# Output weights of group A split early and kept in DRAM, their bounds loaded elsewhere, y stored a unit later, the bias mask laid out on the host

## The chip, the cores and the metric

One core of a Trainium2 chip runs the whole program. Its engines work side by side: TensorE (PE) for matrix products, VectorE (DVE), ScalarE (ACT) and GpSimd (POOL) for elementwise work, and SyncE (SP), whose queue issues nearly all transfers of this kernel, in order. The metric is the device time of one execution, in microseconds (us); lower is better.

## The reference

A hybrid attention block with an MLP, for one sequence of 1024 tokens of width 1024, in float32:

```python
n = rms_norm(x, norm1_g)
qa, ka, va, qb, kb, vb = split(n @ w_in)      # widths 512, 128, 128, 512, 512, 512
ya = mixer_a(...)   # 8 heads of 64 on 2 kv heads, window of 3 chunks of 64, ALiBi, learned sinks
yb = mixer_b(...)   # 8 heads of 64, own chunk and the 8 before it,
                    # plus a learned bias by clipped relative position; else NEG_INF
y = concatenate([rms_norm(ya, out_norm_a_g), rms_norm(yb, out_norm_b_g)])
h = x + y @ w_out
u = square(relu(rms_norm(h, norm2_g) @ w_ff1))
return rms_norm(h + u @ w_ff2, final_norm_g)
```

## The kernel before, in words

**Products.** Data are float32. For a product each operand is split into a high and a low piece of a narrower type, and `mm3` makes the product from three matmuls (high with high, high with low, low with high). Splitting a tile is one ACT row for the high piece (a copy to the narrow type) and one DVE or POOL row for the low one (source minus high). Where the narrow type is f16, the operand is first scaled by a power of two, worked out from a bound on its largest element.

**Attention units.** The first 390 us are input projections, attention and the output projection of group A. Attention runs as 32 units in a fixed order, numbered n: A0_0, A0_2, ... A3_6 (n = 0 to 15; four head pairs, each with four units of two token blocks), then B0_0, B1_0, B0_1, B1_1 (n = 16 to 19), B2_0 (n = 20) and so on to B7_0, B6_1, B7_1 (n = 29, 30, 31; head and half of the tokens). Each unit makes scores (`S_B`; in group A `S_A`), takes exponentials (`P_A`, `P_B`, with `nm_` the negated row maxima from DVE and `sm_` the sums), turns them around (in A by PE transposes `pt_A`, copied by ACT and DVE into `T_A`; in B by a transposing DMA from `H_B`, the pieces of P, into `G_B`) and multiplies by V (`av_A`, `av_B`; the sums go to `Y`). Between the units' matmuls a filler puts the matmuls of the input projections of later heads (`ip_kB`, `ip_qB`, `ip_vB`), and during the last B units those of the output projection of group A (`op_A`). Heads of group B come in pairs: kB1, qB1, vB1 are the projections of pair 1 (heads 2 and 3), KkB, QqB and VvB their keys, queries and values with both pieces.

**Buffers and order.** Weights land in a ring of three load buffers (`stage`, tag "ws"): names `st_qB1`, `bo0` and so on are such buffers. Split pieces (`w0_` high, `w1_` low) and other large tiles live in a ring of 33 pages (`page`). PE's order is written out by the program (`pe` chains every matmul to the one before). The order on the other engines, and on SP, is chosen by the scheduler of the tile framework, which simulates the program; it may move a row ahead of or behind where the program states it. Transfers wait on SP for their buffer and their source, and what stands behind a waiting transfer on SP waits too.

**Output weights.** `w_out` has eight blocks of 128 rows, m = 0 to 3 for group A and 4 to 7 for group B. For the scale of its f16 pieces the kernel needs each row's sum of squares: `bound_weights(m)` loads block m into `bo{m}`, at the start of unit n = m + 2 (`BOUND_AT`), and at the start of the unit after it ACT squares and sums it (L970). `scale_of_weights(0)` turns the sums of group A into a scale at unit B2_0 (DVE rows, and one PE transpose `all_o0` through a PSUM buffer), `scale_of_weights(1)` those of group B at B7_0. `out_weight(m)` loads the block again (`st_o{m}`) and splits it into `w_o{m}` by two ACT rows (L1004) and two DVE rows (L1005); blocks 0 to 3 at the start of the output projection of group A, 4 to 7 in the last unit.

**y.** A finished half of a pair's Y is scaled into f16 pieces (ACT and POOL) and, for pairs 0 to 5, stored to DRAM at once (`yd`). `load_y(m)` brings both token halves back in one transfer of 512 KB ahead of the output projection.

**Bias of group B.** `bias_b[s]` (names `b_B0`, `b_B1`) holds a head's band of biases, 128 x 640. It is loaded (`load_bias`) and then two 64 x 64 corners are set to NEG by POOL (`mask_bias`, L707 and L708), eight times each. DVE adds it to the scores (L660, L662).

## Time and profile before

| | |
|---|---|
| median of 3 runs | 1057.29 us (1055.38 to 1059.46) |
| the profiled execution | 1060.3 us |
| its span | 1058.5 us |
| PE busy | 1004.1 us, 95% of the span |
| DVE, ACT, POOL busy | 72%, 67%, 41% |
| granted TensorE clock, mean | 0.98 |

In the rows of the timeline a line reads: start, duration, engine, line of the kernel, operation, output <- inputs with sizes, count, and in brackets how long the engine stood idle before it and what it waited for. Buffer numbers are left out there: `w_qB` is any of w0_qB0 to w1_qB3. PEld is the weight load of TensorE, which runs beside its matmuls. DMA issues stand under SPq with the time their issue took; from there to landing it takes some microseconds more.

### The profile page before, as it was taken

Reading aid. Unit: us, or ns where it says so; the run is one execution under the profiler, and the core shown is the slowest. Engines: PE = TensorE matmul, PEld = TensorE weight load, DVE = VectorE, ACT = ScalarE, POOL = GpSimd, SP = SyncE. Lnnn points to the kernel's source line nnn. Section 1 sums busy time; section 2 is a strip of 40 time slices with the busy share of each in tenths; the row PEclk is TensorE's granted clock in tenths of the full one; section 3 lists DMA queues with packets and bytes.
Section 4 is the critical chain, followed back from the end, with each engine's and each line's share of the span. In section 5 each row is a group of like instructions: output and inputs, shape, how many; then the busy total and the mean of one; then the engine's idle time right before and its main releaser. Section 6 shows DMA issues by size and latency. Waiting matters only on the chain.

```text
span 1058.5 us, 14063 instructions
## 1 busy us (share of the span) xinstructions
PE 1004.1 (95%) x4821; PEld 566.8 (54%) x4821; DVE 758.4 (72%) x1296; ACT 704.4 (67%) x1118; POOL 432.2 (41%) x324
## 2 busy tenths in 40 slices
...
GB/s 353 259 201 152 130 96 123 198 206 186 203 247 237 164 268 120 120 21 139 200 290 257 183 244 248 186 203 272 242 334 384 219 159 140 178 139 120 1 1 159
DMA packets 150279, 200.63 MB, mean 190 GB/s; under 512 B 78656, under 2 KB 96192, under 8 KB 150208
## 3 DMA queue, kind: packets, MB, share of 16 engines
...
q8 instruction: 38, 0.62, 0.2%
q14 instruction: 33, 0.27, 0.1%
...
## 4 chain that ended last, share of the span: by engine, by line
PE 35%; ACT 9%; DVE 9%; issue 5%; DMA 4%; POOL 2%; SPq 0%; DVEq 0%; ACTq 0%; POOLq 0%
PE f_a L174 13%; PE f L174 8%; PE f_c L174 7%; PE f_b L174 4%; PE op_B L174 2%; POOL W L1428 2%; DMA u<-ud 2%; ACT w L1393 1%; DVE T L1400 1%; DMA m<-in_w_ff_dram 1%; ACT W L1426 1%; DVE X L1316 1%; ACT k L1490 1%; DVE tops_w L1208 1%; ACT k L1489 1%
## 5 line engine op out<-in xcount | busy, mean ns | idle before, releaser
L174 PE MATMUL f<-X,W 128*128 128x512 f16 x1344 | 297.2, 383 | 7.0 <-POOL W L1428 4.8
L174 PEld LDWEIGHTS <-U 128*128 128x128 f16 x1356 | 133.1, 98 | 166.3 <-issue 9.0
L174 PEld LDWEIGHTS <-W 128*128 128x128 f16 x1344 | 132.1, 99 | 168.0 <-POOL W L1428 7.9
L1428 POOL TENSOR_TENSOR U<-u,U 128x1024 f16<-128x1024 f32 x48 | 116.5, 2437 | 173.8 <-ACT U L1426 159.8
L174 PE MATMUL f_a<-V,U 128*128 128x512 f16 x756 | 165.3, 379 | 1.0 <-DVE C L1743 1.0
L1428 POOL TENSOR_TENSOR W<-T,W 128x1024 f16<-128x1024 f32 x29 | 67.9, 2344 | 88.3 <-ACT W L1426 88.3
L1428 POOL TENSOR_TENSOR W<-w,W 128x1024 f16<-128x1024 f32 x21 | 51.6, 2456 | 98.6 <-ACT W L1426 98.6
L174 PE MATMUL f_c<-V,U 128*128 128x512 f16 x384 | 86.5, 386 | 5.5 <-DVE V L1430 3.4
L1424 ACT ACTIVATE u<-u,uup 128x1024 f32<-128x1024 f32 x48 | 53.9, 1141 | 56.1 <-DMA u<-ud 55.9
L1430 DVE SCALAR_TENSOR_TENSOR V<-Z,up,V 128x1024 f16<-128x1024 f32 x32 | 51.4, 1610 | 28.7 <-ACT V L1426 18.5
L663 ACT ACTIVATE P_B<-P_B,nm_B 128x640 f32<-128x640 f32 (+2 forms) x64 | 44.3, 692 | 40.2 <-DVE nm_B L660 23.5
L1426 ACT ACTIVATE U<-u 128x1024 f16<-128x1024 f32 x48 | 50.2, 1046 | 28.1 <-DVE Z L1400 10.8
L901 DVE SCALAR_TENSOR_TENSOR H_B<-P_B,rc_B,H_B 128x640 f16<-128x640 f32 (+2 forms) x64 | 51.3, 823 | 14.3 <-ACT H_B L896 13.9
L174 PEld LDWEIGHTS <-y 128*128 128x128 f16 x384 | 36.6, 100 | 41.8 <-DVE ts_vB L477 3.6
L174 PE MATMUL ip_kB<-nT,w_kB 128*128 128x512 f32 x192 | 54.9, 412 | 2.0 <-POOL w_kB L180 1.3
L1430 DVE SCALAR_TENSOR_TENSOR V<-w,up,V 128x1024 f16<-128x1024 f32 x24 | 42.5, 1771 | 19.7 <-ACT V L1426 15.6
L174 PE MATMUL ip_qB<-nT,w_qB 128*128 128x512 f32 x192 | 55.3, 415 | 1.2 <-ACT P_B L663 1.2
L174 PE MATMUL op_A<-w_o,y 128*128 128x512 f16 x192 | 51.5, 395 | 3.4 <-DVE ts_vB L477 3.4
L174 PE MATMUL S_B<-KkB,QqB 128*128 128x320 f32 (+2 forms) x192 | 44.1, 339 | 10.4 <-DVE nm_B L662 6.8
L174 PE MATMUL ip_qA<-nT,w_qA 128*128 128x512 f32 x192 | 52.8, 411 | 0.3 <-DVE VA L180 0.3
L174 PE MATMUL ip_vB<-nT,w_vB 128*128 128x512 f32 x192 | 51.2, 400 | 0.0
L1426 ACT ACTIVATE V<-Z,up 128x1024 f16<-128x1024 f32 x32 | 36.5, 1139 | 21.6 <-DVE Z L1400 19.4
...
## 6 DMA issues: line engine op xcount, KB each, us to landing
w<-in_w_ff_dram SPq DMA_DIRECT2D x64, 512.0 KB, 7.0
u<-ud SPq DMA_DIRECT2D x56, 512.0 KB, 5.4
ud<-k SPq DMA_DIRECT2D x48, 512.0 KB, 3.1
m<-in_w_ff_dram SPq DMA_DIRECT2D x32, 512.0 KB, 6.0
...
xr<-in_x_dram SPq DMA_DIRECT2D x8, 512.0 KB, 8.7
bo<-in_w_out_dram SPq DMA_DIRECT2D x8, 512.0 KB, 3.5
st_o<-in_w_out_dram SPq DMA_DIRECT2D x8, 512.0 KB, 4.8
```

The lines of the kernel that those rows point to most:

```text
L174: pe(nc.tensor.matmul(*args, **kw))
L663: nc.scalar.activation(pr, pr, AF.Exp, bias=nm, scale=-1.0, accum_out=sm)
L901: nc.vector.scalar_tensor_tensor(lo, q, rc, hi, ALU.mult, ALU.subtract)
L1208: nc.vector.tensor_reduce(self.column(), flat(src), mybir.AxisListType.X, ALU.max, apply_absolute_value=True)
L1316: engine.tensor_tensor(lo, src, hi, ALU.subtract)
L1393: nc.scalar.activation(w, w, AF.Copy, scale=up1)
L1400: engine.tensor_tensor(t, a, b, op)
L1424: nc.scalar.activation(full, full, AF.Copy, scale=up)
L1426: nc.scalar.activation(w[0], full, AF.Copy, scale=1.0 if up is None else up)
L1428: engine.tensor_tensor(w[1], full, w[0], ALU.subtract)
L1430: engine.scalar_tensor_tensor(w[1], full, up, w[0], ALU.mult, ALU.subtract)
L1489: nc.scalar.activation(v, v, AF.Relu, scale=down1[n])
```

## The change

- **Bounds.** Blocks 0 to 3 are loaded at n = 3 to 6 (`BOUND_A`), 4 to 7 at n = 13 to 16 (`BOUND_B`), and squared at the start of the unit two later.
- **Pieces of group A.** Their largest bound is found at n = 9 and the scale at n = 10 (`SPREAD_A`). Blocks 0 to 3 are loaded again at n = 9 to 12 (`PIECES_A`, buffers `so{m}`), split two units later, and the pieces stored to DRAM (`wod`, 512 KB a block) one unit after that. The output projection loads them (`w_r{m}`) instead of loading and splitting `st_o0` to `st_o3`. Blocks 4 to 7 are split as before.
- **Scale of group B.** The bound at B7_0, the scale at B6_1, one unit later.
- **y.** Its store is issued a unit later; the second half of the tokens is loaded at the second token block of the output projection instead of with the first.
- **Mask.** The corners are NEG in the band that the host lays out; the 16 rows on POOL go.

```diff
@@ -50,8 +50,8 @@
 Y_UP, Y_DOWN, O_UP = 13, 14, 12
-BOUND_AT = 2
-SPREAD_B = "B7_0"
+BOUND_A, PIECES_A, BOUND_B = 3, 9, 13
+SPREAD_A, SPREAD_B = (9, 10), ("B7_0", "B6_1")
 PAD = 40
@@ -246,6 +246,7 @@
     yd = dram([6, P, 2, 2, HALF], "yd", F16)
+    wod = dram([4, P, 2, D], "wod", F16)
     hB = [dram([P, 2, D], f"hB{n}") for n in range(TB // 2)]
@@ -273,10 +274,14 @@
-    def bits_over(cols, name, psum, tag, bufs, least):
+    def top_over(cols, name):
...
         nc.vector.tensor_reduce(top, cols, mybir.AxisListType.X, ALU.max)
+        return top
+    def bits_over(top, name, psum, tag, bufs, least):
         spread = psum.tile([P, P], F32, tag=tag, bufs=bufs, name=f"all_{name}")
@@ -672,7 +677,14 @@
-    sq = {}
+    sq, late = {}, []
+    def issue_late(units):
+        while late and late[0][0] >= units:
+            late.pop(0)[1]()
+        for work in late:
+            work[0] += 1
@@ -690,7 +702,6 @@
                     self.load_bias(s)
-                    self.mask_bias(s)
                     continue
@@ -702,10 +713,6 @@
             self.bias.append(bias_b[s])
-        def mask_bias(self, s):
-            nc.gpsimd.memset(bias_b[s][:HD, 5 * P - HD :], NEG)
-            nc.gpsimd.memset(bias_b[s][HD:, :HD], NEG)
@@ -728,7 +735,7 @@
             if self.y is None:
-                nc.sync.dma_start(yd[self.m, :, t], y)
+                late.append([0, lambda: nc.sync.dma_start(yd[self.m, :, t], y)])
             if by_act:
@@ -864,21 +871,18 @@
                 defer.pop(0)[1]()
-            if b % 2:
-                self.next_bias(b == 1)
+            if b == 1:
+                self.next_bias()
             if b % 2:
...
-        def next_bias(self, load):
+        def next_bias(self):
             s, j = 1 - self.s, self.pair.j + self.s
...
                 return
-            if load:
-                pairs_b[j].load_bias(s)
-            else:
-                pairs_b[j].mask_bias(s)
+            pairs_b[j].load_bias(s)
@@ -904,6 +908,8 @@
         def step(self, n):
+            if n == 2:
+                issue_late(0)
             self.apply(self.kbs[n])
@@ -942,32 +948,82 @@
-        e = bits_over(topA, "yA", aps, "w", 2, -50)
+        e = bits_over(top_over(topA, "yA"), "yA", aps, "w", 2, -50)
         power(upA, e, -1.0, 254 + Y_UP)
...
-    def scale_of_weights(group):
+    def factors(group):
         c = slice(4 * group, 4 * group + 4)
+        return c, (gains if group else ogc)[:, c]
+    def top_of_weights(group):
+        c, g = factors(group)
         t = small.tile([P, 4], F32, tag="wbound", bufs=2, name=f"wbound{group}")
-        g = ogc[:, c]
         if group:
-            g = gains[:, c]
             nc.vector.tensor_tensor(og2[:, c], g, g, ALU.mult)
         nc.vector.tensor_tensor(t, wsq[:, c], og2[:, c], ALU.mult)
-        e = root_of_bits(bits_over(t, f"o{group}", aps, "w", 2, -80))
+        return top_over(t, f"o{group}")
+    def scale_of_weights(group, top):
+        c, g = factors(group)
+        e = root_of_bits(bits_over(top, f"o{group}", aps, "w", 2, -80))
         up = scale_tile("oup", str(group), 2)
...
+    def load_wout(m, name):
+        st = stage([P, D], f"{name}{m}")
+        load(st, w_out[m * P : (m + 1) * P, :])
+        return st
     def bound_weights(m):
-        st = stage([P, D], f"bo{m}")
-        load(st, w_out[m * P : (m + 1) * P, :])
+        st = load_wout(m, "bo")
         return lambda: nc.scalar.activation(st, st, AF.Square, accum_out=wsq[:, m : m + 1])
+    def split_weights(m, st):
+        w = page([P, 2, D], f"w_o{m}", F16)
+        g = gains[:, m : m + 1]
+        for j in range(2):
+            c = slice(j * HALF, (j + 1) * HALF)
+            in_turn("o", nc.scalar.activation(w[:, 0, c], st[:, c], AF.Copy, scale=g))
+            nc.vector.scalar_tensor_tensor(w[:, 1, c], st[:, c], g, w[:, 0, c], ALU.mult, ALU.subtract)
+        return w
+    def pieces_of_weights(m):
+        st = load_wout(m, "so")
+        def split():
+            w = split_weights(m, st)
+            later.append(lambda: nc.sync.dma_start(wod[m], w))
+        return split
+    later, ahead2 = [], []
+    def weights_chores(n):
+        if later:
+            later.pop(0)()
+        if ahead2 and ahead2[0][0] <= n:
+            ahead2.pop(0)[1]()
+        for at, m0, work in ((BOUND_A, 0, bound_weights), (PIECES_A, 0, pieces_of_weights), (BOUND_B, 4, bound_weights)):
+            if 0 <= n - at < 4:
+                ahead2.append((n + 2, work(m0 + n - at)))
+        if n == SPREAD_A[0]:
+            tops_o[0] = top_of_weights(0)
+        if n == SPREAD_A[1]:
+            scale_of_weights(0, tops_o[0])
+    tops_o = {}
@@ -990,19 +1046,19 @@
         y = page([P, 2, 2, HALF], f"y_{m}", F16)
-        nc.sync.dma_start(y, yd[m])
+        nc.sync.dma_start(y[:, 0], yd[m, :, 0])
         return y
+    def load_rest(m, y):
+        nc.sync.dma_start(y[:, 1], yd[m, :, 1])
     def out_weight(m):
-        st = stage([P, D], f"st_o{m}")
-        w = page([P, 2, D], f"w_o{m}", F16)
-        load(st, w_out[m * P : (m + 1) * P, :])
-        g = gains[:, m : m + 1]
-        for j in range(2):
-            c = slice(j * HALF, (j + 1) * HALF)
-            in_turn("o", nc.scalar.activation(w[:, 0, c], st[:, c], AF.Copy, scale=g))
-            nc.vector.scalar_tensor_tensor(w[:, 1, c], st[:, c], g, w[:, 0, c], ALU.mult, ALU.subtract)
+        if m < 4:
+            w = page([P, 2, D], f"w_r{m}", F16)
+            nc.sync.dma_start(w, wod[m])
+        else:
+            w = split_weights(m, load_wout(m, "st_o"))
         return w[:, 0], w[:, 1]
@@ -1091,6 +1147,9 @@
         for tb in range(TB):
+            if tb == 1:
+                for m in range(4):
+                    load_rest(m, ys[m])
             h = hres[tb] = page([P, D], f"h{tb}", F32)
@@ -1150,20 +1209,22 @@
             scale_of_y()
-    bound = None
     for n, (unit, name, n_fill) in enumerate(units):
-        if bound is not None:
-            bound()
-        bound = bound_weights(n - BOUND_AT) if 0 <= n - BOUND_AT < 8 else None
+        if unit.name[0] == "A" or n == 16:
+            issue_late(1)
+        weights_chores(n)
         if unit.name == "B2_0":
-            scale_of_weights(0)
             rA = group_rstd("A", aps, "w", 2, None)
-        if unit.name == SPREAD_B:
-            scale_of_weights(1)
+        if unit.name == SPREAD_B[0]:
+            tops_o[1] = top_of_weights(1)
+        if unit.name == SPREAD_B[1]:
+            scale_of_weights(1, tops_o[1])
         ahead.remove(unit)
...
                 ys.append(load_y(m) if m < 6 else y67[m - 6])
+                if m < 6:
+                    load_rest(m, ys[-1])
                 ws.append(out_weight(m))
@@ -1904,6 +1965,8 @@
     band = np.stack([ext[:, 127 - p : 127 - p + 640] for p in range(128)], axis=1)
+    band[:, :64, 576:] = NEG
+    band[:, 64:, :64] = NEG
     d = -np.abs(128 + np.arange(128)[:, None] - np.arange(256)[None, :]).astype(np.float32)
```

What the scheduler makes of it at three places. First ACT, around the square of bo0 (`T_A0_0_0` is the first copy of turned probabilities; before, then now):

```order
L413 ACTIVATE ts_qA1_0_688<-ts_qA1_0_688 128x512
L970 ACTIVATE bo0_933,wsq_184<-bo0_933 128x1024
L231 ACTIVATE w0_qA3_811<-st_qA3_810 128x1024
L663 ACTIVATE P_A0_2_1_714,sm_A0_2_668<-P_A0_2_1_714,nm_A0_2_667 128x256 x2
L789 ACTIVATE es_A0_2_723<-nm_A0_2_667,psink_83 128x2
L670 ACTIVATE T_A0_0_0_742<-pt_A0_0_0_741 128x256
L670 ACTIVATE T_A0_0_1_751<-pt_A0_0_1_750 128x512
```

```order
L418 ACTIVATE ts_qA1_0_689<-ts_qA1_0_689 128x512
L231 ACTIVATE w0_qA3_812<-st_qA3_811 128x1024
L668 ACTIVATE P_A0_2_1_715,sm_A0_2_669<-P_A0_2_1_715,nm_A0_2_668 128x256 x2
L796 ACTIVATE es_A0_2_724<-nm_A0_2_668,psink_83 128x2
L988 ACTIVATE bo0_1039,wsq_185<-bo0_1039 128x1024
L675 ACTIVATE T_A0_0_0_743<-pt_A0_0_0_742 128x256
L675 ACTIVATE T_A0_0_1_752<-pt_A0_0_1_751 128x512
```

The square stands three rows further back, still right ahead of T_A. On SP the load of st_kB0 (wk of pair 0) now stands ahead of bo0's, where it stood behind it; each of bo1 to bo3 is loaded into a buffer that the bo before it held.

Second SP where the A units end (VvB0 are the values of pair 0, KkB1x the keys of pair 1, G_B0_0 the turned pieces of unit B0_0). Before; st_qB1 and st_vB1 stand 17 and 7 rows ahead of the first row shown:

```order
L130 DMA st_kB2_2394<-in_w_in_dram 128x1024
L731 DMA yd_88<-y1_2_1901 128x1024
L499 DMA_TRANSPOSE VvB0_1925<-hvB0_1922 128x8x64 x4
L130 DMA st_qB2_2558<-in_w_in_dram 128x1024
L731 DMA yd_88<-y0_3_2100 128x1024
L467 DMA KkB12_2157<-t1_kB1_2028 64x1024 x2
L467 DMA KkB13_2158<-t1_kB1_2028 64x1024 x2
L467 DMA KkB10_2155<-t0_kB1_2029 64x1024 x2
L467 DMA KkB11_2156<-t0_kB1_2029 64x1024 x2
L904 DMA_TRANSPOSE G_B0_0_2128<-H_B0_0_1_2186 128x6x128
L904 DMA_TRANSPOSE G_B0_0_2128<-H_B0_0_3_2230 128x14x128
L904 DMA_TRANSPOSE G_B1_0_2245<-H_B1_0_1_2284 128x6x128
```

Now, in two pieces that follow one another but for row wod of block 3:

```order
L738 DMA yd_88<-y1_2_1919 128x1024
L504 DMA_TRANSPOSE VvB0_1942<-hvB0_1939 128x8x64 x4
L130 DMA st_qB1_1961<-in_w_in_dram 128x1024
L1006 DMA wod_89<-w_o1_1948 128x2048
L130 DMA bo4_2049<-in_w_out_dram 128x1024
L1006 DMA wod_89<-w_o2_2044 128x2048
L130 DMA bo5_2149<-in_w_out_dram 128x1024
L130 DMA st_vB1_2204<-in_w_in_dram 128x1024
```

```order
L472 DMA KkB12_2194<-t1_kB1_2062 64x1024 x2
L908 DMA_TRANSPOSE G_B0_0_2169<-H_B0_0_1_2223 128x6x128
L472 DMA KkB13_2195<-t1_kB1_2062 64x1024 x2
L472 DMA KkB10_2192<-t0_kB1_2063 64x1024 x2
L738 DMA yd_88<-y0_3_2134 128x1024
L130 DMA bo6_2271<-in_w_out_dram 128x1024
L472 DMA KkB11_2193<-t0_kB1_2063 64x1024 x2
L130 DMA bo7_2378<-in_w_out_dram 128x1024
L908 DMA_TRANSPOSE G_B0_0_2169<-H_B0_0_3_2267 128x14x128
L908 DMA_TRANSPOSE G_B1_0_2287<-H_B1_0_1_2326 128x6x128
L908 DMA_TRANSPOSE G_B1_0_2287<-H_B1_0_3_2376 128x14x128
```

The load of st_qB1 has come behind VvB0; in its ring it follows so1 (split into w_o1), and bo4 follows it. Both transfers of G_B0_0 had the keys alone ahead of them; the second now has bo6 and bo7 too. On ACT the square of bo4 now stands directly ahead of T_A3_6_0, and those of bo5, bo6 behind it follow one by one among the rows of B0_0 to B0_1.

Third SP at the start of the output projection of group A, before and now:

```order
L904 DMA_TRANSPOSE G_B4_1_3373<-H_B4_1_1_3426 128x20x128
L993 DMA y_0_3496<-yd_88 128x2048
L993 DMA y_1_3505<-yd_88 128x2048
L993 DMA y_2_3514<-yd_88 128x2048
L703 DMA b_B0_597<-in_relb_dram 128x640
L130 DMA st_o3_3516<-in_w_out_dram 128x1024
L904 DMA_TRANSPOSE G_B4_1_3373<-H_B4_1_3_3475 128x20x128
L993 DMA y_3_3523<-yd_88 128x2048
L130 DMA st_o4_4239<-in_w_out_dram 128x1024
L130 DMA st_o5_4248<-in_w_out_dram 128x1024
L464 DMA QqB30_3412<-t0_qB3_3408 64x512
L464 DMA QqB31_3413<-t0_qB3_3408 64x512
```

```order
L908 DMA_TRANSPOSE G_B4_1_3394<-H_B4_1_1_3446 128x20x128
L1059 DMA w_r0_3510<-wod_89 128x2048
L1049 DMA y_0_3512<-yd_88 128x1024
L1059 DMA w_r1_3514<-wod_89 128x2048
L1049 DMA y_1_3516<-yd_88 128x1024
L1059 DMA w_r2_3518<-wod_89 128x2048
L1049 DMA y_2_3520<-yd_88 128x1024
L1059 DMA w_r3_3522<-wod_89 128x2048
L1049 DMA y_3_3524<-yd_88 128x1024
L908 DMA_TRANSPOSE G_B4_1_3394<-H_B4_1_3_3496 128x20x128
L714 DMA b_B0_598<-in_relb_dram 128x640
L908 DMA_TRANSPOSE G_B5_1_3533<-H_B5_1_1_3567 128x20x128
```

G_B4_1's second transpose and b_B0 have come behind all eight loads, where three loads stood ahead of b_B0. The loads st_o4 to st_o6 stand far ahead now, where st_o0 to st_o2 stood. Of y, `128x2048` has become `128x1024`; the other halves follow some ten rows below, between b_B1 and h1 (rows of x for the residual).

## The prediction

> **What bounds the kernel now.** I read the page's first part, then the list of all waits of PE, then windows by stage, then the timeline of each engine around the waits found.
>
> The page, busy time and share of the span:
>
> ```profile
> PE 1004.1 (95%) x4821; PEld 566.8 (54%) x4821; DVE 758.4 (72%) x1296; ACT 704.4 (67%) x1118; POOL 432.2 (41%) x324
> ```
>
> PE is the bound: 1004.1 of a span of 1058.5, so about 54 us is all that any change of waits can bring, and the change leaves PE's matmuls as they are (their order too, but for one small transpose). The question is which of PE's waits go and which new ones come. PE's waits between 40 and 400 us (total, times, longest):
>
> ```profile
> PE S_B L174 <- DVE nm_B L662: 6.8, 2, 5.4
> PE av_A L174 <- ACT T_A L670: 5.2, 2, 3.5
> PE S_B L174 <- DVE nm_B L660: 3.6, 3, 1.5
> PE op_A L174 <- DVE ts_vB L477: 3.4, 1, 3.4
> PE av_A L174 <- DVE T_A L180: 2.0, 3, 0.9
> PE ss_A L174 <- DVE t_qB L449: 1.3, 1, 1.3
> PE ip_qB L174 <- ACT P_B L663: 1.2, 1, 1.2
> ```
>
> Four of these rows (5.2, 3.6, 3.4 and the 5.4 in 6.8) lie at places that the change touches. The stages, as busy time of each engine in a window (PE, PEld, DVE, ACT, POOL, granted clock, DMA share, GB/s):
>
> ```profile
> 140.00:160.00 20.00, 17.96 (x93) 14.93 (x91) 13.82 (x43) 12.21 (x36) 14.92 (x16) 0.91 0.32 92
> 160.00:180.00 20.00, 17.93 (x97) 14.83 (x96) 14.23 (x38) 13.83 (x36) 13.74 (x14) 1.00 0.33 82
> 180.00:200.00 20.00, 19.12 (x101) 15.53 (x100) 16.30 (x42) 15.17 (x35) 9.28 (x9) 1.00 0.91 193
> 300.00:320.00 20.00, 15.55 (x76) 11.26 (x74) 15.52 (x28) 13.35 (x25) 1.50 (x4) 1.00 1.09 253
> ```
>
> Work is added to the first three, where PE has little slack and ACT is 41.2 of 60 us busy; it is taken from the last, where PE idles 4.5 of 20 us and DMA is full.
>
> **The bounds of the output weights (squares of bo).** Where they stand, on SP, ACT and PE (start, duration, in brackets the idle time before):
>
> ```profile
> 50.28 0.52 SPq L130 DMA_DIRECT2D bo<-in_w_out_dram  x1
> 50.91 0.38 SPq L130 DMA_DIRECT2D st_kB<-in_w_in_dram  x1
> 55.07 1.06 ACT L970 ACTIVATE bo<-bo 128x1024 f32<-128x1024 f32 x1 [5.59 <-DMA bo<-in_w_out_dram]
> 58.66 0.38 PE L174 MATMUL av_A<-T_A,VA 128*128 128x256 f32 x1 [3.48 <-ACT T_A L670]
> 59.79 0.39 PE L174 MATMUL av_A<-T_A,VA 128*128 128x256 f32 x1 [0.75 <-DVE T_A L180]
> 81.14 1.06 ACT L970 ACTIVATE bo<-bo 128x1024 f32<-128x1024 f32 x1 [2.69 <-DMA bo<-in_w_out_dram]
> 85.74 0.38 PE L174 MATMUL av_A<-T_A,VA 128*128 128x256 f32 x1 [1.69 <-ACT T_A L670]
> 86.46 0.62 PE L174 MATMUL av_A<-T_A,VA 128*128 128x256 f32 x3 [0.34 <-DVE T_A L180]
> ```
>
> bo4 to bo7 leave this part of the program altogether. ACT's wait of 2.69 for bo4 goes, and with it the 1.69 + 0.34 = 2.0 us that PE waits four microseconds later: **−2.0** (nothing if another row holds T_A there; I see none). For bo0 the change does less than its words: the scheduler still sets bo0's square right ahead of the T_A copy, only three ACT rows further on, and SP now loads st_kB0 ahead of bo0, so that bo0 lands after 57 instead of 55. Square and T_A then end about where they did: **0**. All of 3.48 + 0.75 = 4.2 could go if bo0 landed as before; the loss if bo1 to bo3, each now loaded only after the square before it, hold ACT in turn is about 1.5 (a late landing of some 2 us, less the rows that run meanwhile).
>
> **The boundary between A and B (150 to 200 us).** What the added pieces cost (count, busy, mean ns):
>
> ```profile
> L1005 DVE SCALAR_TENSOR_TENSOR w_o<-st_o,gains_o,w_o 128x512 f16<-128x512 f32 x16 | 14.8, 966 | 5.6 <-ACT w_o L1004 5.6
> L1004 ACT ACTIVATE w_o<-st_o,gains_o 128x512 f16<-128x512 f32 x16 | 10.3, 713 | 4.0 <-DMA st_o<-in_w_out_dram 4.0
> L970 ACT ACTIVATE bo<-bo 128x1024 f32<-128x1024 f32 x8 | 8.4, 1056 | 8.8 <-DMA bo<-in_w_out_dram 8.7
> L970 ACT ACTIVATION_READ_ACCUMULATOR bo<-bo 128x1 f32 x8 | 1.5, 186 | 0.0
> ```
>
> Eight halves at 0.71 and four squares at 1.06 + 0.19 put 5.7 + 5.0 = 10.7 us on ACT, and eight at 0.97 put 7.7 us on DVE: ACT goes from 41.2 to about 52 of 60, DVE from 44.4 to 52. That fits only if nothing waits, and SP gets twelve transfers of 512 KB (so, wod, bo) in a ring of three load buffers. The rows there now:
>
> ```profile
> 165.47 5.26 SPq L499 DMA_TRANSPOSE VvB<-hvB  x4
> 169.37 1.05 ACT L231 ACTIVATE w_qB<-st_qB 128x1024 fp32r<-128x1024 f32 x1
> 170.50 2.96 POOL L180 TENSOR_TENSOR w_qB<-st_qB,w_qB 128x256 fp32r<-128x256 f32 x4 [1.31 <-ACT w_qB L231]
> 175.79 0.94 PE L174 MATMUL ip_qB<-nT,w_qB 128*128 128x512 f32 x3 [1.17 <-ACT P_B L663]
> 178.70 7.36 SPq L467 DMA_DIRECT2D KkB<-t_kB  x8
> 182.27 0.60 ACT L670 ACTIVATE T_A<-pt_A 128x512 fp32r<-128x512 f32 x1
> 186.16 5.86 SPq L904 DMA_TRANSPOSE G_B<-H_B  x3
> 193.85 0.33 PEld L174 LDWEIGHTS <-VvB 128*128 128x128 f16 x4 [0.27 <-DMA G_B<-H_B]
> st_qB<-in_w_in_dram SPq DMA_DIRECT2D x1, 512.0 KB, 3.6
> ```
>
> Three things are late here. First st_qB1: before it is loaded long ahead; now it stands on SP behind the VvB0 transposes, whose issue ends at 165.47 + 5.26 = 170.7, and it waits for DVE's last piece of w_o1, because that frees its buffer: issue at 172 to 175, I take 173.7. It lands 3.6 later, ACT needs 1.05 and POOL a quarter of 2.96: the first ip_qB could start at 173.7 + 3.6 + 1.05 + 0.74 = 179.1 where it starts at 175.79: +3.3. Second bo4, which waits for POOL's last quarter of w_qB1 (173.7 + 3.6 + 1.05 + 2.96 = 181.3), lands 3.6 later and is squared by 186.2; it stands ahead of T_A on ACT, due at 182.27 + 3.3 = 185.6: +0.7. Third G_B0_0_3: now behind all KkB copies, bo6 and bo7, and bo6 and bo7 wait for the squares of bo4 and bo5. I put its issue at 194, and a like transpose's landing 5 to 6 us later (issue of three takes 5.86), at 199.5, where av_B with that shift is due at 193.85 + 3.5 or so = 197.4: +2. Sum **+6.0**. The ends: 0, if w_o1 is split early enough for st_qB1 to land by 174; 11, if st_qB1 costs its 3.3, bo4 a whole wait as it does now (2.7) and G_B0_0_3 a whole landing (5). I take the middle since PE's order is fixed, and what is late on ip_qB can't be filled.
>
> The store of y one unit later and the store of the pieces keep nobody waiting but SP: the pieces are read back 120 us later. The scale's transposing matmul, 128x128, sits now among the A units: nothing.
>
> **200 to 300 us.** Group A's scale leaves unit B2_0. Its transposing matmul took one of the two PSUM buffers there, so that ss_A had to wait 1.3 for t_qB to read the other: **−1.3**; ends 0 (what is late shifts to the next matmul) and −2.7 (with the 1.4 that is left of the row of 6.8, in this stretch too).
>
> **Out projection of A (303 to 344 us).** The rows that set its end:
>
> ```profile
> 307.09 1.46 SPq L993 DMA_DIRECT2D y<-yd  x3
> 311.98 6.08 SPq L904 DMA_TRANSPOSE G_B<-H_B  x1
> 322.54 2.28 PE L174 MATMUL op_A<-w_o,y 128*128 128x512 f16 x6 [3.40 <-DVE ts_vB L477]
> 339.48 0.57 SPq L703 DMA_DIRECT2D b_B<-in_relb_dram  x1
> 343.09 0.14 POOL L707 MEMSET b_B<- 64x64 f32 x1 [1.76 <-DMA b_B<-in_relb_dram]
> 343.26 0.29 DVE L662 CUSTOM_DVE_ANT_0 P_B<-S_B,b_B 128x128 f32<-128x128 f32 x1 [5.20 <-POOL b_B L707]
> 343.62 1.01 PE L174 MATMUL S_B<-KkB,QqB 128*128 128x384 f32 x2 [5.43 <-DVE nm_B L662]
> ```
>
> PE waits 3.6 + 3.4 + 5.4 = 12.4 us here. The splits of w_o0 to w_o3 (5.7 us of ACT, 7.7 of DVE) leave, so the 3.6 and the 3.4, which are waits for DVE, shrink. But a PE that comes sooner only waits longer for b_B1: DVE stood 5.20 before 343.26, so it would have taken the bias at 338. What counts is when b_B1 lands, and ahead of it SP is without a gap. Between G_B4_1_1 and b_B1 stood four y and four st_o, 8 x 512 KB = 4.2 MB; now four w_r and four halves of y, 3.1 MB. A megabyte less at 253 GB/s is 4.2 us, and the bias's two memsets (0.3) go. Against it: G_B4_1_3 and b_B0, which stood behind three y, are now behind the whole 3.1 MB (12.4 us from 307, so landing at 320 to 322, where PE, 3 to 5 us sooner, wants G_B4_1_3): 1.5 back. **−3.0**; ends 0 and −11 (if b_B1 comes before it is wanted, and all but the first 1.4 of the 12.4 goes). The second halves of y, 1 MB ahead of h1, have a token block's 24 matmuls of some 0.38 us, with scores between, as cover.
>
> SP is solid there, and the Trainium skill (Perfetto Trace Analysis, "What 'DMA-bound' means") says that an issuing engine with solid DMA slices is making descriptors, not moving data. By that rule the number of transfers counts, which is eight before and eight after, the saved megabyte is worth nothing, and the sum would come out 3 us higher. The trace speaks against it: one G_B transpose holds SP 6.08 us here and three hold it 5.86 at 186.16, so its length follows what is queued ahead.
>
> **Sum.** −2.0 + 0 + 6.0 − 1.3 − 3.0 = −0.3. The profiled execution took 1060.3 (its span 1058.5 and 1.8 around it), 3.0 above the median of 1057.29; the same step on the median gives 1057.0.
>
> **Rivals.** (a) *Faster: the out projection runs free.* With DVE and ACT unloaded, b_B1 not only lands 4 us sooner but before PE wants it, and that stretch gives 8 instead of 3, while the boundary takes 3: −2.0 + 3 − 1.3 − 8 = −8.3, 1049. For it: all five waits there end on engines whose work is removed or on SP's queue. Against it: DMA share 1.09. (b) *Slower: the boundary is not absorbed.* ACT at 52 of 60 us with squares that wait for their loads, st_qB1 and G_B0_0_3 late, and the out projection gives back only the memsets: −2.0 + 11 − 1.3 − 0.3 = +7.4, 1064.7. It decides from about 9 us lost at the boundary. Against it: DMA share 0.33 from 140 to 180, room for the loads. (c) *The bounds are not moved in effect:* T_A waits as before for whatever bo stands ahead of it, at 55 and again at 81: +2.0 + 1.5 over the likeliest, 1060.5. The order of ACT speaks for it at bo0, not at bo4. (d) *Number, not bytes, sets SP's pace in the out projection:* the −3.0 goes, 1060.0; spoken against by the 6.08.
>
> **How the numbers follow.** Half a per cent, 5.3 us, is about what can be told from no change. Likeliest 0.30 (own range 1053 to 1062, one or two of its terms off by half), (c) 0.05, (d) 0.08: same 0.43. (a) 0.29: faster. (b) 0.28: slower. For 8 in 10 the range must take in most of (a) and (b) about their values: 1048 to 1066; ends beyond (boundary 0 and out projection −11: 1043) are left out.
>
> **What would show it.** Right: no ACT wait for bo at 81; an ip_qB of B1 behind POOL or ACT w_qB by 2 to 4 us near 177; an av_B behind G_B near 198; b_B1 landing near 339, PE resuming some 3 us sooner against its own matmuls. Wrong: PE without a wait from 170 to 200 (then 1051), no wait on b_B1 (a), or ACT without idle time and PE waiting for T_A from 150 to 200 (b).

## The result, and the profile after

The change made the kernel slower: 1070.56 us median of 4 runs (1065.45 to 1071.76) against 1057.84 of the kernel before, a ratio of 1.0113 [1.0074, 1.0153]. That is 4.6 us beyond the upper end of the predicted range. The profiled execution took 1071.76 (its span 1070.0), against 1060.3 (1058.5). Ratios here and below leave out two single runs of far greater length, one of the kernel before (1719 us) and one of buffers_only (3681 us).

PE's busy time in the page's first part, of the kernel after:

```profile
PE 1008.0 (94%) x4821; PEld 569.5 (53%) x4821; DVE 758.5 (71%) x1296; ACT 705.0 (66%) x1118; POOL 436.3 (41%) x308
```

The number of matmuls is unchanged, but PE is busy 3.9 us longer (1008.0 against 1004.1). So of the 11.5 us that the span grew, 7.6 are waits and 3.9 are the same matmuls running longer. The waits of PE between 40 and 400 us, kernel after (total, times, longest):

```profile
PE S_B L174 <- DVE nm_B L667: 8.3, 4, 6.0
PE av_B L174 <- DMA G_B<-H_B: 5.7, 1, 5.7
PE av_A L174 <- ACT T_A L675: 5.6, 2, 5.1
PE ip_qB L174 <- ACT w_qB L231: 5.3, 1, 5.3
PE S_B L174 <- DVE nm_B L665: 2.2, 2, 1.5
PE op_A L174 <- DVE ts_vB L482: 2.1, 1, 2.1
```

Two rows are new and large, `av_B` behind G_B and `ip_qB` behind w_qB. The 6.0 in the first row is the wait for b_B1, which was to shrink. The timeline of the kernel after, around the boundary of A and B, on the engines in turn:

```profile
173.57 0.53 SPq L130 DMA_DIRECT2D st_qB<-in_w_in_dram  x1
178.07 1.06 ACT L231 ACTIVATE w_qB<-st_qB 128x1024 fp32r<-128x1024 f32 x1 [1.86 <-DMA st_qB<-in_w_in_dram]
179.18 1.67 PE L174 MATMUL ip_qB<-nT,w_qB 128*128 128x512 f32 x3 [5.29 <-ACT w_qB L231]
181.76 4.45 DVE L997 SCALAR_TENSOR_TENSOR w_o<-so,gains_o,w_o 128x512 f16<-128x512 f32 x3
187.16 1.71 SPq L472 DMA_DIRECT2D KkB<-t_kB  x2
189.57 0.50 PE L174 MATMUL S_B<-KkB,QqB 128*128 128x256 f32 x2 [0.97 <-DVE nm_B L667]
191.44 1.00 PE L177 MATMUL pt_A<-ident,P_A 128*128 128x128 f32 x4 [1.37 <-DVE T_A L180]
197.44 1.08 SPq L130 DMA_DIRECT2D bo<-in_w_out_dram  x1
201.19 8.94 SPq L908 DMA_TRANSPOSE G_B<-H_B  x3
209.90 0.91 PE L174 MATMUL av_B<-G_B,VvB 128*128 128x384 f16 x3 [5.69 <-DMA G_B<-H_B]
```

Three waits follow one another: for the late st_qB1, for DVE (held by three low rows of w_o in a row), and for G_B0_0_3 (the row at 201.19), issued behind the copies of KkB1, bo6 and bo7 (bo7 at 200.18). The first ip_qB stood at 175.79 before, so it is 3.4 late; the av_B that waits, the second of its unit, stood at 193.92 and is 16.0 late. The waits alone do not give that. What stands beside them is the granted clock, in windows of the kernel after cut along it (PE, PEld, DVE, ACT, POOL, clock, DMA share, GB/s):

```profile
171.00:177.80 6.80, 2.89 (x18) 2.18 (x16) 5.00 (x13) 3.44 (x10) 1.89 (x2) 1.00 0.78 176
177.80:184.60 6.80, 5.42 (x16) 4.38 (x17) 4.13 (x6) 5.04 (x9) 5.34 (x6) 0.51 0.25 73
184.60:191.40 6.80, 4.50 (x22) 3.31 (x20) 6.52 (x12) 4.24 (x10) 3.89 (x3) 0.99 1.00 349
191.40:194.80 3.40, 3.37 (x11) 2.79 (x12) 0.55 (x4) 3.40 (x9) 0.00 (x0) 0.53 1.33 188
194.80:208.20 13.40, 8.87 (x43) 6.93 (x42) 8.72 (x23) 8.53 (x19) 4.04 (x5) 0.99 1.06 233
208.40:215.20 6.80, 5.30 (x16) 4.25 (x15) 3.93 (x8) 4.57 (x8) 3.38 (x3) 0.52 1.09 285
```

After each wait the clock stands at half for 3.4 or 6.8 us, while PE has work. The same six matmuls of ip_qB show it in the timeline, before and then after:

```profile
177.28 1.55 PE L174 MATMUL ip_qB<-nT,w_qB 128*128 128x512 f32 x6
```

```profile
181.92 2.76 PE L174 MATMUL ip_qB<-nT,w_qB 128*128 128x512 f32 x6
```

Half of PE's busy time in the three slow windows, (5.42 + 3.37 + 5.30) / 2, is 7.0 us lost. I then set PE's matmuls of the two traces against each other one by one, in their common order (4819 of 4821), and took how much later each starts after the change:

| at (us, before) | 40 | 70 | 80 | 100 | 170 | 180 | 190 | 200 | 240 | 300 | 330 | 343 | 400 | end |
|---|---|---|---|---|---|---|---|---|---|---|---|---|---|---|
| later by (us) | -0.9 | 1.0 | 2.4 | -1.8 | -0.7 | 6.0 | 9.3 | 18.5 | 15.3 | 13.6 | 9.9 | 10.4 | 12.4 | 11.1 |

So the boundary costs 19.2 (from -0.7 to 18.5). Added waits are 11.6 of it: 5.29 - 1.17, 0.97, 1.37 - 0.8, 0.53 for another nm_B, and 5.69 - 0.27. The clock is 7.0 more, as this trace splits the time; the run fill_the_wait below qualifies that. By 300 4.9 us have come back, and 3.2 more from 300 to 343. The end of the output projection of group A, on SP, DVE and PE of the kernel after:

```profile
339.94 5.18 SPq L504 DMA_TRANSPOSE VvB<-hvB  x4
345.22 0.53 SPq L1154 DMA_DIRECT2D h<-in_x_dram  x1
345.80 4.17 SPq L908 DMA_TRANSPOSE G_B<-H_B  x1
350.01 0.58 SPq L714 DMA_DIRECT2D b_B<-in_relb_dram  x1
353.71 0.29 DVE L667 CUSTOM_DVE_ANT_0 P_B<-S_B,b_B 128x128 f32<-128x128 f32 x1 [6.63 <-DMA b_B<-in_relb_dram]
354.06 1.01 PE L174 MATMUL S_B<-KkB,QqB 128*128 128x384 f32 x2 [6.00 <-DVE nm_B L667]
```

b_B1 is issued 10.5 us later than before (339.48), behind VvB3, h0 and G_B5_1_3. PE had made up 3.7 us by 330 and stood 6.00 for it instead of 5.43.

### The profile page after: what moved, and what is told of

Read it like the earlier page. It is cut to its first block, busy times and chain, and to the rows that moved or that the text cites. A ratio compares the mean times of both kernels' runs of the same rounds, so it can differ in the third digit from the quotient of the medians.

```text
span 1070.0 us, 14044 instructions
## 1 busy us (share of the span) xinstructions
PE 1008.0 (94%) x4821; PEld 569.5 (53%) x4821; DVE 758.5 (71%) x1296; ACT 705.0 (66%) x1118; POOL 436.3 (41%) x308
## 4 chain that ended last, share of the span: by engine, by line
PE 37%; ACT 7%; issue 7%; DVE 6%; DMA 3%; POOL 3%; SPq 0%; DVEq 0%; POOLq 0%; ACTq 0%
PE f_a L174 13%; PE f L174 9%; PE f_c L174 7%; PE f_b L174 4%; POOL W L1489 3%; PE op_B L174 2%; DMA u<-ud 2%; ACT w L1454 1%; PE op_A L174 1%; DMA w<-in_w_ff_dram 1%; ACT W L1487 1%; DVE tops_w L1269 1%; ACT k L1550 1%; ACT k L1551 1%; DVE V L1491 1%
## 5 line engine op out<-in xcount | busy, mean ns | idle before, releaser
L1489 POOL TENSOR_TENSOR W<-T,W 128x1024 f16<-128x1024 f32 x29 | 70.5, 2434 | 83.6 <-ACT W L1487 83.5
L1491 DVE SCALAR_TENSOR_TENSOR V<-Z,up,V 128x1024 f16<-128x1024 f32 x32 | 48.5, 1517 | 29.5 <-ACT V L1487 22.3
L174 PE MATMUL ip_qB<-nT,w_qB 128*128 128x512 f32 x192 | 57.8, 430 | 5.3 <-ACT w_qB L231 5.3
L1549 DVE CUSTOM_DVE_ANT_0 k<-f,k 128x1024 f32<-128x1024 f32 x24 | 29.3, 1220 | 33.0 <-PE f L174 22.4
L174 PE MATMUL op_A<-w_r,y 128*128 128x512 f16 x192 | 50.1, 388 | 2.1 <-DVE ts_vB L482 2.1
```

The source lines that it names most:

```text
L174: pe(nc.tensor.matmul(*args, **kw))
L1489: engine.tensor_tensor(w[1], full, w[0], ALU.subtract)
L1491: engine.scalar_tensor_tensor(w[1], full, up, w[0], ALU.mult, ALU.subtract)
L1549: dve.tensor_tensor_reduce(v, ps, v, 1.0, 0.0, ALU.add, ALU.max, top)
```

## The experiments

Theories that they had to tell apart: **L**, the late loads at the boundary (bo4 to bo7 and the ring of three load buffers) are what costs; **W**, the added splitting itself, on ACT, DVE and POOL; and, for the output projection, whether b_B1 is late through bytes ahead of it, through its memsets, or through its place on SP. Ratios are to the kernel before, measured beside each group of runs.

**bo_later.** bo4 to bo7 leave the boundary.

```diff
-BOUND_A, PIECES_A, BOUND_B = 3, 9, 13
+BOUND_A, PIECES_A, BOUND_B = 3, 9, 20
```

> The changed kernel with blocks 4 to 7 of the output weights loaded for their bounds at units 20 to 23 instead of 13 to 16; nothing else moves by hand. In the changed kernel PE lost 19 us between 170 and 215 us. Theory L (late transfers, each wait paid again in clock): the wait for w_qB1 (5.3 us, and some 2.7 of half clock behind it) stays, since the pieces stand where they stood; the 5.7 us wait for G_B behind bo6 and bo7 and its half clock (2.7) go, so PE is some 9 to 11 us earlier at 215 us and the time is about 1060. Theory W (the work itself: 10.7 us more on ACT and 7.7 on DVE fill those engines there): only the squares' 5 us move, so at most 5 us come back: 1065 or more.

Measured: 1075.27, 1.0161 [1.013, 1.0192], slower still. PE's waits in its timeline, two at the boundary and one among the units of group B:

```profile
180.85 1.67 PE L174 MATMUL ip_qB<-nT,w_qB 128*128 128x512 f32 x3 [5.53 <-ACT w_qB L231]
207.62 0.54 PE L174 MATMUL av_B<-G_B,VvB 128*128 128x384 f16 x3 [3.53 <-DMA G_B<-H_B]
288.92 0.61 PE L174 MATMUL S_B<-KkB,QqB 128*128 128x384 f32 x2 [2.97 <-DVE nm_B L667]
```

Without bo6 and bo7 ahead of it the wait for G_B falls only from 5.69 to 3.53: G_B0_0_3 is issued at 200.67, hardly sooner than the 201.19 of the changed kernel, because the copies of KkB1 ahead of it begin at 188.81 (187.16 there, 178.70 before the change). The wait for w_qB stays, and where the squares now stand, among units of group B, PE loses 5 us (from 15.0 late at 260 to 20.0 at 275). L as a whole does not hold.

**pieces_at_17.** The pieces of group A leave the boundary for units 17 to 20.

```diff
-BOUND_A, PIECES_A, BOUND_B = 3, 9, 13
+BOUND_A, PIECES_A, BOUND_B = 3, 17, 13
```

> The changed kernel with the pieces of group A loaded at units 17 to 20 (split at 19 to 22) instead of 9 to 12; the bounds of blocks 4 to 7 stay at 13 to 16. Theory L: st_qB1 is loaded early again, PE starts ip_qB of pair 1 without the 5.3 us wait and without the half clock behind it, and bo4 to bo7, loaded sooner, are no longer ahead of the second G_B0_0 transpose: the boundary loses 0 to 3 us, not 19. The pieces now burden 200 to 260 us, where PE is full: 0 to 5 there. Time 1052 to 1059. Theory W: the splits' 5.7 us of ACT and 7.7 of DVE cost the same wherever PE is full, and the squares stay: 1064 or more.

Measured: 1070.81, 1.0114 [1.0087, 1.014]. The boundary costs 7.0 us (from -1.9 at 160 to 5.1 at 200) instead of 19, but 7 come in from 220 to 330, during and after the splitting. Two waits of PE:

```profile
168.66 0.38 PE L174 MATMUL av_A<-T_A,VA 128*128 128x256 f32 x1 [3.75 <-ACT T_A L675]
317.19 0.90 PE L174 MATMUL av_B<-G_B,VvB 128*128 128x384 f16 x3 [3.73 <-DMA G_B<-H_B]
```

The work is not free in either place, and bo4 and bo5 ahead of T_A cost a wait of their own.

**pieces_early.** Everything moved: bounds of A a unit earlier, pieces at units 6 to 9, bounds of B after the boundary.

```diff
-BOUND_A, PIECES_A, BOUND_B = 3, 9, 13
-SPREAD_A, SPREAD_B = (9, 10), ("B7_0", "B6_1")
+BOUND_A, PIECES_A, BOUND_B = 2, 6, 20
+SPREAD_A, SPREAD_B = (6, 7), ("B7_0", "B6_1")
...
-                ahead2.append((n + 2, work(m0 + n - at)))
+                ahead2.append((n + 1 + (at != BOUND_A), work(m0 + n - at)))
```

> The changed kernel with the bounds of group A loaded at units 2 to 5 and squared one unit later as before the change, the scale at units 6 and 7, the pieces loaded at 6 to 9 and split at 8 to 11, and blocks 4 to 7 bounded at 20 to 23. On SP st_qB1 then stands well ahead of VvB0, and no bo among the G_B. Theory L: no wait of PE above 2 us between 170 and 215, the boundary costs 0 to 2 us, and what the changed kernel won back later (some 6 us between 215 and 345) is kept: about 1050, 1046 to 1055. Theory W: the same ACT and DVE work now sits between 95 and 170 us, where PE is as full: PE waits for T_A there, 1060 or more.

Measured: 1075.55, 1.0151 [1.0117, 1.0184]. The boundary costs only 5.3 (from -0.8 at 170 to 4.5 at 200), yet PE loses some 11 us from 215 to 275, in waits for DVE of 3.6, 2.4 and 1.6 beside the squares of bo4 to bo7, and at a granted clock of 0.83 from 240 to 260. The expectation fell: the boundary is not the only place without room.

**fill_the_wait.** Ten matmuls of zeros ahead of the first ip_qB of pair 1, in the 5.29 us that PE waits there: they change no result.

```diff
+DUMMY = 10
...
+            if name == "qB1" and t == 0:
+                for m in range(DUMMY):
+                    matmul(acc, zero.to_broadcast([P, P]), zero.to_broadcast([P, HALF]), start=m == 0, stop=m == DUMMY - 1)
```

> The changed kernel with ten matmuls of zeros (128x512, about 4.1 us) put on PE directly ahead of the first ip_qB of pair 1, into the same PSUM buffer, which that matmul overwrites: PE is busy during most of the 5.3 us that it waits there for w_qB. If the clock is halved because PE stood idle, the half clock from 178 to 185 us goes and the ip_qB matmuls behind it take 0.43 us each, not 0.86: 2 to 3 us less at 190 us, and a time of 1067 to 1069. If the half clock has another cause, it stays and the time stays at 1070 to 1071.

Measured: 1069.71, 1.0109 [1.0083, 1.0135]. PE's rows:

```profile
175.52 2.45 PE L175 MATMUL ip_qB<-zero 128*128 128x512 f32 x10 [1.81 <-DVE t_kB L457]
179.03 1.38 PE L175 MATMUL ip_qB<-nT,w_qB 128*128 128x512 f32 x3 [1.05 <-ACT w_qB L232]
206.41 0.91 PE L175 MATMUL av_B<-G_B,VvB 128*128 128x384 f16 x3 [2.52 <-DMA G_B<-H_B]
```

The ten matmuls took 2.45 us and not the 4.1 expected, since such matmuls start 0.23 us apart at full clock (0.43 at half). The real product starts where it did (179.03 against 179.18), but the half clock at 178 is gone: the clock's record stays at full from 158 to 189. That shows that the half clock follows from PE's idling and not from the work beside it. It does not show that this half clock cost its 2.7 us. The 2 to 3 us expected at 190 did not come: PE is 9.8 late there, against 9.3 in the changed kernel, because it now waits 2.85 for nm_B and 1.85 for T_A on DVE, where it waited 0.97 and 1.37. DVE was not ready any sooner. At 200 PE is 13.9 late instead of 18.5, but through G_B0_0_3: the scheduler had put bo7 behind it, it was issued at 198.18 instead of 201.19, and PE waits 2.52 for it instead of 5.69. The gain is lost again further on, and the time cannot be told from that of the changed kernel.

**y_and_mask.** From the kernel before: the store of y a unit later, y loaded in halves, the mask in the host's band. Bounds, scales and pieces as before.

```diff
-                    self.mask_bias(s)
-                nc.sync.dma_start(yd[self.m, :, t], y)
+                late.append([0, lambda: nc.sync.dma_start(yd[self.m, :, t], y)])
-        nc.sync.dma_start(y, yd[m])
+        nc.sync.dma_start(y[:, 0], yd[m, :, 0])
+    band[:, :64, 576:] = NEG
+    band[:, 64:, :64] = NEG
...
```

> The kernel before with two parts of the change alone: y stored a unit later and its second half loaded at the second token block, and the mask laid out with the bias. Weights as before. Both theories: nothing changes up to 300 us. In the output projection of group A one megabyte less stands ahead of b_B1, two memsets fewer follow it: 2 to 4 us, 1054 to 1056. If the number of transfers sets the pace of that stretch and not their bytes: 1057 to 1058.

Measured: 1053.68 (8 runs), 0.9951 [0.9927, 0.9975], just below the 1054 to 1056 expected. On SP and PE:

```profile
327.46 0.53 SPq L709 DMA_DIRECT2D b_B<-in_relb_dram  x1
329.52 5.78 SPq L499 DMA_TRANSPOSE VvB<-hvB  x4
324.64 2.74 PE L174 MATMUL op_A<-w_o,y 128*128 128x512 f16 x6 [3.71 <-DVE ts_vB L477]
```

b_B1 goes out 12 us sooner than before, ahead of VvB3, and the wait of 5.43 is gone. The wait for ts_vB stays.

**bias_soon_before.** Is that bytes, memsets, or place? The kernel before, with the load of each bias moved up only; y and memsets untouched.

```diff
-            if b % 2:
-                self.next_bias(b == 1)
+            if b == 3:
+                self.next_bias(True)
+            if b == 1:
+                self.next_bias(False)
...
+            if load:
+                if self.t == 1 and self.pair.j < 3:
+                    pairs_b[self.pair.j + 1].load_bias(self.s)
+                return
...
-            if self.s != self.t or j in (0, 4):
-                return
...
+            if self.s == self.t and j not in (0, 4):
```

> The kernel before with the loads of the biases alone moved up: b_B1 ahead of st_o6, the VvB3 transposes, h0 and G_B5_1_3. Masks, y and weights as before. If the place of b_B1 is what y and the mask gained by, the 5.4 us wait at 343 goes: 1052 to 1054. If the megabyte of y or the memsets gained: 1057 to 1058.

Measured: 1053.46, 0.9946 [0.9925, 0.9968]; b_B1 goes out at 327.30, and no wait for it is left. The place alone gives all that y and the mask give.

**bias_first** and **bias_first_before.** The same from the other side: in the kernel after (and in the one before), the load of the bias is stated a block earlier and held ahead of the transfer that stood right before it on SP, one place up.

```diff
-            nc.sync.dma_start(bias_b[s], relb[2 * self.j + s])
+            after(nc.sync.dma_start(bias_b[s], relb[2 * self.j + s]), "bias")
...
-            nc.sync.dma_start_transpose(self.G[:, o : o + w], H[:, : w * P])
+            after(nc.sync.dma_start_transpose(self.G[:, o : o + w], H[:, : w * P]), None, "bias")
```

> The changed kernel with each load of a bias placed on SP ahead of the next transposing G_B transfer, so that the last b_B1 stands one place earlier, ahead of G_B5_1_3 (whose issue took 4.2 us). Nothing else moves. If the place of b_B1 on SP sets the end of the output projection's first part, PE's wait of 6.0 us at 354 shrinks to about 2 and the half clock behind it with it: 4 to 6 us less, 1065 to 1067. If DMA's bytes or PE's own work set it: unchanged, 1070.

> The kernel before with one edit: the last b_B1 is put on SP one place earlier, ahead of G_B5_1_3. No mask, no y, no weights changed. If the place of b_B1 is what the change of y gained by (it moved b_B1 three places up), PE's 5.4 us wait at 343 shrinks to 1 to 2 us and its half clock goes: 3 to 5 us less, 1053 to 1055. If the gain of that run came from the bytes of y or from the memsets: 1057 to 1058.

Measured: 1068.74, 1.0092 [1.0057, 1.0127], and 1057.6, 0.9999 [0.9984, 1.0013]. One place is too little: the wait goes from 6.00 to 3.97 and from 5.43 to 3.64.

**after_bias_soon** and **y_mask_bias_soon.** Each bias loaded as soon as its buffer is free, in the kernel after and in y_and_mask.

```diff
-            if b == 1:
+            if b == 3:
...
-            s, j = 1 - self.s, self.pair.j + self.s
-            if self.s != self.t or j in (0, 4):
-                return
-            pairs_b[j].load_bias(s)
+            j = self.pair.j + 1
+            if self.t == 1 and j < 4:
+                pairs_b[j].load_bias(self.s)
```

> The changed kernel with each bias loaded as soon as its buffer is free: b_B1 now stands ahead of the VvB3 transposes, h0 and G_B5_1_3 (together 10 us of issue), b_B0 ahead of the eight loads. Place of b_B1 sets the stretch: the 6.0 us wait at 354 goes and with it up to 3.4 us of half clock: 1062 to 1065. If the bytes ahead or the removed splits set it: 1070. Either way the 19 us of the boundary stay.

> The kernel with y and the mask changed and no weights changed, and each bias of group B now loaded as soon as the last scores that read its buffer are through; on SP b_B0 stands three places higher, b_B1 where it stood. PE had no wait for b_B1 left in that kernel, so nothing or 1 us: 1052 to 1054. It is the candidate that beats both kernels.

Measured: 1065.53, 1.0066 [1.0042, 1.009]; and 1052.65 (8 runs), 0.9938 [0.9918, 0.9959], the lowest median of the versions that compute the reference, though it cannot be told from y_and_mask and bias_soon_before; all three beat both kernels. In the kernel after a wait of 2.95 for G_B at 351 takes part of the place of the 6.00.

**bounds_moved_only.** y_and_mask, with the bounds where the change puts them, squared two units on.

```diff
-BOUND_AT = 2
+BOUND_A, BOUND_B = 3, 13
...
+        for n0, m0 in ((BOUND_A, 0), (BOUND_B, 4)):
+            if 0 <= n - n0 < 4:
+                bounds.append((n + 2, bound_weights(m0 + n - n0)))
```

> The kernel with y and the mask changed, and of the weights only the bounds: blocks 0 to 3 at units 3 to 6, 4 to 7 at units 13 to 16, each squared two units later; no pieces, so weights are split in the output projection as before. From the runs so far: 3 to 4 us gained at 75 to 90, and at 165 to 170 some 6 lost to bo4 and bo5, whose squares stand ahead of T_A (seen with the pieces at units 17 to 20): about 1056 (1052 to 1060). If it is the pieces alone that cost at the boundary: 1050.

Measured: 1058.17 (10 runs), 0.9997 [0.998, 1.0015], 4.5 above y_and_mask. PE gains 3.8 at 80 to 90, where bo4 stood, and loses 5.1 at 160 to 170, where it stands now; 2.3 more go before that gain, from 70 to 80, beside bo0 to bo3. ACT's row of bo5's square, and PE's two waits:

```profile
166.59 1.06 ACT L972 ACTIVATE bo<-bo 128x1024 f32<-128x1024 f32 x1 [2.32 <-DMA bo<-in_w_out_dram]
170.09 0.58 PE L174 MATMUL av_A<-T_A,VA 128*128 128x256 f32 x1 [2.20 <-ACT T_A L670]
172.13 1.01 PE L174 MATMUL av_A<-T_A,VA 128*128 128x256 f32 x3 [1.46 <-DVE T_A L180]
```

A square that waits for its load stands ahead of T_A on ACT again, in another place.

**pieces_bounds_as_before.** The kernel after with the bounds back where they were, pieces at 10 to 13.

```diff
-BOUND_A, PIECES_A, BOUND_B = 3, 9, 13
+BOUND_A, PIECES_A, BOUND_B = 2, 10, 6
...
-                ahead2.append((n + 2, work(m0 + n - at)))
+                ahead2.append((n + 1 + (work is pieces_of_weights), work(m0 + n - at)))
```

> The changed kernel with all eight bounds loaded and squared where they were before the change (units 2 to 9, one unit later), and the pieces at units 10 to 13 (at 9 the ring of load buffers locks up). So y, mask and pieces changed, bounds not. By the ladder so far (y and mask -4, bounds +4.5, pieces +12), if the parts add up: about 1066 (1063 to 1069). If the pieces cost only together with bo4 to bo7 at the boundary: 1054 to 1058.

Measured: 1065.74, 1.0068 [1.0041, 1.0094]. The parts add up. Taken from the ratios to the kernel before, y and mask make -5.2 us, the bounds +4.9 and the pieces +12.4, together +12.1, where the whole change makes +12.0.

**so_pages** and **so_bo_pages.** Is it the ring of three load buffers that makes st_qB1 late? From after_bias_soon, `so` (then `bo` too) is loaded into the ring of 33 pages.

```diff
-        st = stage([P, D], f"{name}{m}")
+        st = (page if name == "so" else stage)([P, D], f"{name}{m}", F32)
```

> The changed kernel with early biases (1065.5), and the blocks that are split early loaded into the 33 pages instead of the ring of three load buffers; every load, split and store stays. On SP st_qB1 stands far ahead of VvB0 again. If the ring is what costs: no wait for w_qB at 179 (5 us and the half clock behind it), though ACT may wait for bo4 and bo5 ahead of T_A at 168 as it did with the pieces at unit 17: 1056 to 1061. If the added work costs: 1064 to 1067.

> The same with the bounds' blocks in pages too. If the ring is what costs, both the wait for w_qB and T_A's wait behind bo4 and bo5 go, and the kernel comes near the one without any change of weights: 1052 to 1057. If the added ACT and DVE work costs: 1063 to 1067.

Measured: 1069.52, 1.0097 [1.0071, 1.0123], and 1065.99, 1.0069 [1.0044, 1.0094]: no gain (after_bias_soon had 1.0066), and the theory fell as it was put. ACT and PE in so_pages:

```profile
185.86 1.06 ACT L231 ACTIVATE w_qB<-st_qB 128x1024 fp32r<-128x1024 f32 x1 [1.68 <-DMA VvB<-hvB]
186.97 1.65 PE L174 MATMUL ip_qB<-nT,w_qB 128*128 128x512 f32 x3 [8.96 <-ACT w_qB L231]
```

The split of st_qB1 now waits for the VvB0 transposes: w0_qB1 comes into the page that held hvB0, which they read. Four more tiles in the page ring turn it on by four, and the wait only changes its name.

**work_only** and **buffers_only.** The two halves of the pieces apart, each added to y_mask_bias_soon at the boundary: eight copies in place on ACT and as many on DVE, on a bias tile that is loaded at unit 11 for it, without further loads or buffers; then four loads through the ring with their pages, of which only eight columns are split.

```diff
+        if 12 <= n < 16:
+            for _ in range(2):
+                b = bias_b[1][:, :HALF]
+                a = nc.scalar.activation(b, b, AF.Copy, scale=ones)
...
+                nc.vector.scalar_tensor_tensor(b, b, ones, b, ALU.mult, ALU.max)
```

```diff
+            w = page([P, 2, D], f"w_e{m}", F16)
+            in_turn("o", nc.scalar.activation(w[:, 0, :8], st[:, :8], AF.Copy, scale=ident[:, :1]))
+            nc.vector.scalar_tensor_tensor(w[:, 1, :8], st[:, :8], ident[:, :1], w[:, 0, :8], ALU.mult, ALU.subtract)
...
+            st = stage([P, D], f"so{n - 10}")
+            load(st, w_out[(n - 10) * P : (n - 9) * P, :])
```

> The kernel with y, mask and early biases (1052.65) plus eight copies of 128x512 on ACT and eight on DVE at units 12 to 15, in place on the bias that waits there, where the changed kernel splits the early pieces; they change no value, load and store nothing and take no buffer. If the added work is what the early pieces cost: a loss of 7 to 10 us between 150 and 215, 1060 to 1063. If buffers and transfers cost: 1052 to 1055.

> The same kernel plus the four early loads of group A's blocks through the ring at units 10 to 13 and a page for each one's pieces, as with the pieces at these units, but only eight columns of each half are split and nothing is stored or read back; the output projection loads and splits as before. On SP st_qB1 stands behind VvB0. If buffers and transfers cost: 8 to 11 us lost between 170 and 215, 1061 to 1064. If the work costs: 1053 to 1055.

Measured: 1058.26 (10 runs), 0.9991 [0.9974, 1.0008], so +5.6 on y_mask_bias_soon; and a ratio of 1.0026 [1.0001, 1.0052], about +9 (the median of the four runs that count is 1061.8). From 160 to 200 us PE loses 5.1 and 5.7 against y_mask_bias_soon, where the pieces of pieces_bounds_as_before lose 10.0 against y_and_mask: both halves cost, and at the boundary they add up. Over the whole time they do not: 5.6 and 9 are more than the 12 of the pieces, and buffers_only loses 2 us more from 215 to 300. In work_only ip_qB waits 2.70, for ACT's P_B, with w_qB1's split only 1.0 later than before (170.36 against 169.37). In buffers_only, with next to no splitting, PE waits 1.15 for nm_B and 2.14 for T_A on DVE, and the windows show slow matmuls:

```profile
180.00:200.00 20.00, 16.71 (x74) 13.47 (x73) 14.43 (x34) 12.99 (x30) 6.91 (x8) 0.83 0.96 230
```

Against 19.12 and x101 before: 3.3 us are idle, and a sixth of the clock is withheld.

**one_split.** What could the pieces have given at most? From y_mask_bias_soon, blocks 1 to 3 use the pieces of block 0: three loads and splits are left out of the computation and nothing is added elsewhere.

```diff
+        if 0 < m < 4:
+            return first_w_o[0]
...
+        first_w_o.append((w[:, 0], w[:, 1]))
```

> The kernel with y, mask and early biases (1052.65) with the loads and splits of blocks 1 to 3 left out: the output projection of group A takes block 0's pieces for all four, so it computes something else, with as many matmuls. It shows the most that taking the splits out there can gain. If the waits of PE for DVE at 305 to 325 (1.4, 0.6, 1.5 and 3.7 us) come from the splits: 1045 to 1048. If they come from DVE's other work and PSUM buffers: 1050 to 1053.

Measured: 1048.93, 0.9905 [0.9878, 0.9932], 3.7 below y_mask_bias_soon. The waits in its output projection:

```profile
PE op_A L174 <- ACT o L1120: 3.9, 1, 3.9
PE S_B L174 <- DVE nm_B L660: 2.1, 3, 1.3
PE op_A L174 <- DVE ts_vB L477: 1.4, 1, 1.4
```

The wait for ts_vB falls from 4.0 to 1.4; those for nm_B stay in part (2.1 of 3.6), so the splits are not their only cause. By its matmuls PE is 5.9 us ahead of y_mask_bias_soon at 330, and has lost that again by 350, to the new wait of 3.9 for ACT and the half clock behind it. So three quarters of the removed work are worth 5.9 us in that stretch and 3.7 in the end, and the two intervals overlap, so that even the 3.7 is not certain. The change paid 12 for it.

## Why the prediction was wrong

The side was that of rival (b), which had 0.28, and whose condition (9 us lost at the boundary) was met by far; the likeliest case was wrong. By its steps:

- **Bounds, 40 to 100 us: predicted -2.0 and 0, measured -0.9 (from -0.9 at 40, ahead of the first of these loads, to -1.8 at 100).** bo4's wait at 81 is gone, as said, and PE gains 3.8 from 80 to 90: the 2.0 of waits, and the 3.4 us of half clock that stood right behind them before (87.5 to 90.9). bo0 turned out as rival (c) had it for that place: PE waits 5.14 for T_A where it waited 3.48. That the sum is only 1.1 off is luck, two errors of opposite sign: bo0 to bo3, taken as 0, cost 3.3 by 80, and bo4 gave about twice what was counted.
- **The boundary: predicted +6.0 with ends 0 and 11, measured +19.2. This is the step that failed.** Its first term was right to a tenth, by luck: st_qB1 issued at 173.57 (said: 173.7), first ip_qB at 179.18 (said: 179.1). What held st_qB1 was not w_o1, whose last row ended at 171.8, but the VvB0 transposes ahead of it, which began 2.7 us later than before and were issued until 173.5. It then took 4.4 us to land, not 3.6, and the first product waited for ACT's piece alone, without the 0.74 counted for POOL. The second named the wrong engine: no wait for T_A behind bo4's square, but 0.97 + 1.37 behind DVE, whose three low rows of w_o took 1.48 us each where 0.97 had been counted. The third was too small, and its cause was mostly another: bo6 and bo7 stood ahead of G_B0_0_3 as said, but took only 2.0 us of SP. It was issued at 201.19, not 194, because the copies of KkB1 ahead of it began 8.5 us later (187.16 against 178.70): the last low piece of kB1 comes from POOL, where it now stood behind the pieces of the late w_qB1 (183.93 against 177.39). So the late st_qB1 is paid for twice. And three such transposes took 8.94, not 5.86. All added waits together, 11.6, are about the end of 11 that I had given. What the sum had no term for is the clock: 7.0 us of matmuls at half speed right behind the waits. By fill_the_wait the first 2.7 of these are no loss of their own, since DVE would have held PE about as long; at that place the sum lacked the wait for DVE as much as the clock. A hint stood in the rows of before: a clock of 0.91 in the window 140 to 160, where the waits were 0.7 to 1.3.
- **200 to 300: predicted -1.3, with an end at -2.7; measured -4.9.** Both waits of that stretch went, ss_A's 1.3 and the 1.4 of nm_B, so the end was the truth for waits. Most of the rest is again the clock. In windows of the kernel before, cut along its half-clock stretches, 3.4 us each:

```profile
241.00:244.40 3.40, 3.40 (x11) 2.75 (x10) 2.07 (x5) 1.48 (x3) 3.37 (x5) 0.52 1.08 209
323.00:326.40 3.40, 3.40 (x11) 1.59 (x10) 3.26 (x15) 1.88 (x5) 0.00 (x0) 0.51 1.02 281
344.00:347.40 3.40, 3.40 (x13) 1.44 (x12) 1.65 (x6) 2.00 (x7) 0.53 (x1) 0.57 1.19 195
```

  The first of them, behind ss_A's wait, is gone after the change: 1.7 more. How much of this the removal from B2_0 earned, and how much a PE that comes 15 us late and so finds others done, no run told apart.
- **Output projection: predicted -3.0, measured -3.2 by the shift from 300 to 343, for other reasons than those given.** The waits add up to 11.1 after and 12.4 before, 1.3 less; the second window above went too, 1.7 more. A megabyte less ahead of b_B1 did not bring it sooner: it was issued 10.5 us later, as late as PE was, behind VvB3, h0 and G_B5_1_3. What stood at 344 for 3.4 us is 6.8 long after (352 to 358.8, clock 0.50), which the shift at 400 shows as 2.0 lost again. bias_soon_before shows that b_B1's place on SP decides, and it saves the whole wait with not a byte less. So the rule of the Trainium skill that was weighed (Perfetto Trace Analysis, "What 'DMA-bound' means") does not settle it either: neither the bytes nor the number of transfers were the question, but which of them the scheduler had put ahead. The 6.08 against 5.86 that was held against the rule compared one transpose of 20 blocks with three of 6, 14 and 6. A fairer pair says the same: G_B0_0_3, of 14 blocks, held SP for 1.99 us before and 5.34 after.
- **What hid the rest.** "Work is added to the first three" windows was counted as 10.7 us of ACT and 7.7 of DVE fitting into idle time, if nothing waits. work_only shows 5.6 us from such work alone, without a load of weights; with PE's order fixed, rows of ACT or DVE that come late become waits of PE.

The range ended at 1066, a little above rival (b), whose 11 us at the boundary gave 1064.7. With 7 us for the clock on top, (b) would have stood at 1071.7, and a range up to it would have held 1070.56.

What stays open: why the waits for nm_B in the output projection remain when three quarters of the splitting go; how much of the pieces' +12 is the order that the scheduler chose rather than the work, since no run held that order fixed; and how much of the 7.0 us at half clock would be left as waits for DVE if PE never slowed down. Each experiment also let the scheduler place the rest anew.
